# Token-major gates and branches, a ready-made convolution table, and a first block without splitting

## The chip, the cores and the metric

The kernel runs on one core of a Trainium2 chip. The metric is the device time of one execution in microseconds (us). The number reported is the median over runs.

## The reference

Two transformer blocks run one after the other on S = 256 tokens of width D = 2048, all in float32. What matters here, cut short:

```python
# first block: three branches, then a feed-forward
gates = sigmoid(gate_logits)                        # gate_logits = columns of rms_norm(x) @ w_in
mixed = (gates[0] * (o_a @ w_branch_a) + gates[1] * (o_b @ w_branch_b)
         + gates[2] * (o_c @ w_branch_c))
x = x + rms_norm(mixed @ w_out, g_post_mix)
h2 = rms_norm(x, g_pre_ffn)
f_gate, f_up = split(h2 @ w_ffn_in)
x = x + rms_norm((silu(f_gate) * f_up) @ w_ffn_out, g_post_ffn)
...
# second block, layer 0: a state-space mixer
h = modulate(rmsnorm(x), shift, scale)
u, z = split(h @ w_in)
x_re, x_im = scan(a_re, a_im, bu_re, bu_im)         # one recurrence per group and state, along tokens
y = einsum(x_re, c_re) - einsum(x_im, c_im) + d_skip * u
y = gelu(y); y = y * sigmoid(y @ w_glu + b_glu)
x = x + gate * ((y * silu(z)) @ w_out)
# second block, layer 1: attention over a shared key/value store
h_kv = modulate(rmsnorm(x), kv_shift, kv_scale); kv = h_kv @ w_kv
h = modulate(rmsnorm(x), shift, scale); proj = h @ w_qg; ...
```

## The kernel before

Nearly all of the work is products of a 256 x K operand with a weight of K x N. A weight is streamed in *units* of 256 rows x 512 columns (512 KB). For each unit, SyncE issues a load into one of four `raw` buffers. ScalarE then rounds it to the matmul's short format (`whi`, L156), and VectorE subtracts that from the original (`wlo`, L157). The activations are held as the same kind of pair (`Act`, parts `hi` and `lo`). A product is three matmuls: hi x hi, hi x lo and lo x hi. There are three `whi` and three `wlo` buffers.

A block is 512 output columns and, for K = 2048, eight units. Two orders exist. In `ws` (L190) the weights are stationary: a unit is 24 matmuls of 256 columns, and the output has the channels on the partitions. In `as_` (L223) the activations are stationary: a unit is 12 matmuls of 512 columns, and the output has the tokens on the partitions. After each unit, `pump` gives a turn to side work, which is written as generators: attention, retention, tables, modulation. The `credit` of a generator says how many steps it takes per unit. `self.late` holds steps that the next `as_` block runs after its second unit (third for K = 2048).

Three norms lie on the way: after the branches (`post_norm`, L830), after the feed-forward (`ffn`, L895, whose result goes to `ssm`) and after the state-space layer (`gated_out`, whose result goes to `nsa`). At each of them the last block or blocks are computed token half by token half (`as_last`, `by_tokens`, L254): in the pass t = 0 over tokens 0 to 127 the units are loaded and most of them kept in large buffers (`kept`), and in the pass t = 1 they are used again. So the norm of the first half can be worked out while the second half is multiplied. `by_tokens` keeps all units but the last three; those use `whi` and `wlo`. The first block after a norm (`as_first`, L301) is also done by halves, and `ready(k, t)` prepares two channel blocks of its operand at a time: transposes on TensorE (`tp`), scaling, and a split into a pair. In that block VectorE is busy with the norm, so GpSimd does the subtraction for the weights (`shared`, and the flag `True` in `as_first`). The factor of a norm is a chain of small VectorE operations on one column (`rstd`, L333 to L341), and in the last two norms also a diagonal matrix `diag` (L363) with which TensorE transposes and scales in one step.

The state-space layer's short convolution uses tables that depend on weights alone. `ssm_tables` makes them as side work during the feed-forward: tiles of `gm` are loaded, multiplied, and written by GpSimd's queue to a DRAM tensor `kern` of 128 groups (L1297, 32 issues). Later `ssm_direct` (L1577) loads 16 tiles of 8 groups with overlapping rows of 128 elements, and GpSimd zeroes what lies in the future by a product with a mask `past` (L1588). In that stretch TensorE computes z, and VectorE also runs the scan, four operations a step (L1545 to L1548).

The order on each engine is set by the tile framework's scheduler, from the order of the code, its own estimate of durations and the waits written as `issue_after`. DMAs go through the queues of SyncE and of GpSimd; within a queue they are issued in order.

## Time and profile before

| | |
|---|---|
| runs | 3265.74, 3266.39, 3269.41 us; median 3266.39 |
| profiled execution | 3265.34 us, of which the span is 3263.2 us |
| mean granted TensorE clock | 0.989 of full speed |
| busy over the span | TensorE 97%, its weight load 86%, VectorE 73%, ScalarE 45%, GpSimd 5% |
| DMA | 744.48 MB, 228 GB/s in the mean |

The span is what the trace covers; 2.1 us lie around it. A busy share is a mean over stages. TensorE's 97% leaves some 97 us in which it waits, and these lie in a few places. Its clock is granted at two levels, so the mean of 0.989 also stands for a few stretches at half speed.

### The profile page before, as it was taken

The numbers are of one execution on the slowest core, as the hardware profiler recorded it, in microseconds if no ns is written. First come the engines' busy times: TensorE is split into PE (matmuls) and PEld (weight loads), VectorE is DVE, ScalarE is ACT, GpSimd is POOL, SyncE is SP. The second block draws the span as 40 slices with busy tenths as digits, with TensorE's granted clock in tenths as the row PEclk, the third lists the DMA queues.
The fourth block names the chain that finished last, engine by engine and source line by source line (L and its number), as shares of the span: only waits on it lengthen the run. The fifth ranks groups of instructions, "written<-read, shape, count | busy, mean of one in ns | idle before, by whom it ended". The sixth has DMA issues, their size and how long they took to land. (4 is left out here: it accounts for less than half of the span.)

```text
span 3263.2 us, 52186 instructions
## 1 busy us (share of the span) xinstructions
PE 3166.2 (97%) x20582; PEld 2812.7 (86%) x20582; DVE 2375.1 (73%) x3580; ACT 1461.9 (45%) x2066; POOL 177.2 (5%) x184
## 2 busy tenths in 40 slices
PE   9999999999999998999999999898899899999998
PEld 8999899988999996887778778677798798899997
DVE  7777676777787766999989956757777865655666
ACT  5544434344344445444434444554444434544444
POOL 0000000000000002000000010303100200000000
PEclk9999999999999999999999999898999999999999
DMA  8868756888777785677777788486788585455574
GB/s 280 260 196 270 237 184 200 255 279 270 223 235 246 249 286 160 213 273 251 262 264 272 253 279 272 139 273 199 232 240 268 170 272 174 135 150 161 143 229 171
DMA packets 438246, 744.48 MB, mean 228 GB/s; under 512 B 29732, under 2 KB 105288, under 8 KB 437104
## 3 DMA queue, kind: packets, MB, share of 16 engines
q1 hardware_dynamic: 428000, 710.45, 68.4%
q0 software_dynamic: 9360, 29.62, 2.6%
q8 instruction: 161, 2.64, 0.3%
q10 hardware_dynamic: 640, 1.07, 0.1%
q14 instruction: 85, 0.70, 0.1%
HBM read 716.80 MB, written 24.24 MB: 227 GB/s over the span
## 5 line engine op out<-in xcount | busy, mean ns | idle before, releaser
L156 ACT CAST whi<-raw 128x1024 fp32r<-128x1024 f32 (+2 forms) x1059 | 1029.5, 981 | 1375.8 <-PE mm L150 1191.3
L157 DVE TENSOR_TENSOR wlo<-raw,whi 128x1024 fp32r<-128x1024 f32 (+2 forms) x1045 | 1181.6, 1139 | 611.3 <-ACT whi L156 600.0
L150 PE MATMUL mm<-act,whi 128*128 128x256 f32 (+1 forms) x8000 | 1485.0, 287 | 3.7 <-ACT whi L156 3.7
L150 PEld LDWEIGHTS mm<-act,whi 128*128 128x128 f32 (+1 forms) x8000 | 1255.5, 193 | 34.7 <-issue 24.3
L150 PE MATMUL mm<-whi,act 128*128 128x512 f32 x3792 | 1185.1, 391 | 5.4 <-ACT whi L156 4.5
L150 PE MATMUL mm<-act,wlo 128*128 128x256 f32 (+1 forms) x4000 | 1143.7, 288 | 7.0 <-DVE wlo L157 6.9
L150 PEld LDWEIGHTS mm<-whi,act 128*128 128x128 f32 x3792 | 711.4, 188 | 160.6 <-issue 7.0
L150 PEld LDWEIGHTS mm<-act,wlo 128*128 128x128 f32 (+1 forms) x4000 | 767.9, 193 | 23.9 <-issue 11.9
L150 PE MATMUL mm<-wlo,act 128*128 128x512 f32 x1896 | 743.9, 393 | 13.6 <-DVE wlo L157 11.6
L150 PEld LDWEIGHTS mm<-wlo,act 128*128 128x128 f32 x1896 | 356.6, 188 | 98.2 <-DVE wlo L157 21.3
L1087 DVE SCALAR_TENSOR_TENSOR acc<-side_raw,c_act,acc 128x512 f32<-128x512 f32 x480 | 359.3, 749 | 23.2 <-DMA side_raw<-mod_w 18.4
L150 PE MATMUL mm<-kept,act 128*128 128x512 f32 x360 | 95.0, 411 | 9.3 <-DVE act L157 9.3
L150 PEld LDWEIGHTS mm<-kept,act 128*128 128x128 f32 x360 | 69.1, 197 | 25.5 <-DVE act L157 10.9
L1273 DVE TENSOR_TENSOR side<-tables,ssm_c 128x512 f32<-128x512 f32 x64 | 65.7, 1088 | 2.3 <-DMA ssm_c<-ssm_c_re 2.3
L1107 POOL DMA_DIRECT2D mod<-side x24 | 12.0, 499 | 959.9 <-ACT side L1106 958.6
L156 ACT CAST kept<-raw 128x1024 fp32r<-128x1024 f32 x30 | 31.2, 1049 | 27.8 <-DMA raw<-w_out 7.4
L1588 POOL TENSOR_TENSOR side_raw<-side_raw,past 128x1024 f32<-128x1024 f32 x16 | 39.5, 2479 | 60.7 <-PE mm L150 33.5
L160 DVE SCALAR_TENSOR_TENSOR act<-tp,vec,act 128x256 fp32r<-128x256 f32 (+1 forms) x64 | 25.4, 413 | 22.3 <-ACT act L159 21.9
L150 PEld LDWEIGHTS tp<-diag,x 128*128 128x128 f32 x192 | 27.7, 205 | 15.1 <-issue 9.8
L150 PE MATMUL tp<-diag,x 128*128 128x128 f32 x192 | 29.0, 292 | 11.3 <-DVE diag L363 9.0
L159 ACT ACTIVATE act<-tp,vec 128x256 fp32r<-128x256 f32 (+1 forms) x64 | 25.5, 418 | 28.2 <-DVE act L160 13.4
L346 ACT ACTIVATE big<-x 128x512 f32<-128x512 f32 x40 | 25.1, 628 | 27.2 <-DVE x L1640 18.5
(378 smaller groups left out, 1929.8 us busy)
## 6 DMA issues: line engine op xcount, KB each, us to landing
raw<-w_in SPq DMA_DIRECT2D x272, 512.0 KB, 4.5
side_raw<-mod_w SPq DMA_DIRECT2D x192, 512.0 KB, 5.2
raw<-w_ffn_in SPq DMA_DIRECT2D x176, 512.0 KB, 5.0
raw<-nsa_w_qg SPq DMA_DIRECT2D x128, 512.0 KB, 3.7
raw<-w_ffn_out SPq DMA_DIRECT2D x88, 512.0 KB, 5.3
side_raw<-kv_mod_w SPq DMA_DIRECT2D x64, 512.0 KB, 4.7
raw<-ssm_w_in SPq DMA_DIRECT2D x64, 512.0 KB, 5.0
raw<-w_kv SPq DMA_DIRECT2D x48, 512.0 KB, 4.4
```

Source lines behind the costliest of these rows:

```text
L150: return self.nc.tensor.matmul(out, lhsT, rhs, start=start, stop=stop, skip_group_check=True).ins
L156: self.last_hi = nc.scalar.copy(hi, src).ins
L157: self.last = (engine or nc.vector).tensor_sub(lo, src, hi.bitcast(F32)).ins
L159: nc.scalar.activation(hi, src, AF.Copy, scale=scale)
L160: self.last_scaled = nc.vector.scalar_tensor_tensor(lo, src, scale, hi.bitcast(F32), op0=OP.mult, op1=OP.subtract).ins
L346: return self.nc.scalar.activation(self.work([128, 512], "big"), x, AF.Square, accum_out=out).ins
L1087: nc.vector.scalar_tensor_tensor(acc, raw[:, k], c, acc, op0=OP.mult, op1=OP.add)
L1107: nc.gpsimd.dma_start(flat[n:n + 4].rearrange("(o k) p -> o (k p)", o=1), row[r])
L1273: nc.vector.tensor_mul(w[i], y[r][:, :, :, None].to_broadcast([128, 4, 8, 16]), x[q][:, :, None, :].to_broadcast([128, 4, 8, 16]))
L1588: nc.gpsimd.tensor_mul(raw, raw, cols(past, 8))
```

## The change

Three parts.

1. `branch` uses `as_` instead of `ws`, for the gates and for the branch products: 160 units. `mixed` becomes two tiles of tokens x 2048 channels instead of channels x tokens. The operand of `w_out` is therefore made by transposes (`transpose_act`), put on `self.late` in the branch that comes last.
2. `as_first` no longer splits anything for its own block. The weights are loaded into large buffers as they are (`kept_raw`; two units use `raw`), the operand is kept unsplit (class `Unsplit`), and each product is one float32 matmul. The split of the operand, which the following blocks need, is done in the pass t = 1 of that block (`rest`). GpSimd splits no weights any more. The two `hold`s on the order of the splits and of the block's weights go away; that on `done` stays. Transposes of the first half are asked for inside `as_last` (`beside`).
3. `kern` holds for each of its 16 rows of a group 112 zeros and the values, so that the masked table can be copied out of it without a mask: 128 new DMAs on GpSimd's queue, one for each group, from `kern` to a DRAM tensor `direct` (64 KB each). `ssm_direct` loads plain tiles of `direct`, and its product with `past` is gone. The loads of `gm` in `ssm_tables` are fetched one ahead.

```diff
     def branch(self, i, o, w, mixed, act=None, done=None):
...
         for b in range(4):
-            ps = self.ws(self.hT, win, GATE + i * D + b * 512)
+            c = slice(b * 512, b * 512 + 512)
+            ps = self.as_(self.hT, win, GATE + i * D + b * 512)
...
-            ps = self.ws(o, wv, b * 512)
...
+            ps = self.as_(o, wv, b * 512)
+            for t in range(2):
+                m, g = mixed[t].t[:, c], gs[t]
...
-                if done is not None:
-                    self.split(done.hi(k, 2), done.lo(k, 2), m, 0.5)
+            if done is not None:
+                self.late.append(partial(self.transpose_act, [m.t[:, c] for m in mixed], done, 4, b * 4, 0.5))
```

```diff
+class Unsplit:
...
+    def rest(self, act):
+
+        def rest(k):
+            while act.n < k + 2:
+                act.grow()
+            self.k.split(act.hi(k, 2), act.lo(k, 2), self.slots[k // 8].t[:, k % 8:k % 8 + 2])
...
-    def as_first(self, act, wv, c0, ready):
+    def as_first(self, x, wv, c0, ready, rest):
...
+        slots, raws = [], []
+        for t in range(2):
             r = slice(t * 128, t * 128 + 128)
+            ready(0, t)
+            for u in range(8):
+                k0 = u * 2
+                if u < 7:
+                    ready(k0 + 2, t)
+                if t == 0:
+                    if u < 6:
+                        if u % 2 == 0:
+                            slots.append(self.slot([128, 2, 2, 512], F32, "kept_raw"))
+                        raw = slots[-1].t[:, u % 2]
+                    else:
+                        raw = self.wp.tile([128, 2, 512], F32, name="raw", bufs=4)
+                    self.nc.sync.dma_start(raw, self.rows_of(wv, k0)[:, :, c0:c0 + 512])
+                    raws.append(raw)
+                for k in range(2):
+                    self.mm(ps[t], x(k0 + k)[:, r], raws[u][:, k], k0 + k == 0, k0 + k == 15)
+                if t:
+                    rest(k0)
```

```diff
-        self.kern = dp.tile([128, 112 + 16 * 128], F32, name="kern")
+
+        self.kern = dp.tile([128, 16, 240], F32, name="kern")
+        self.direct = dp.tile([16, 128, 8, 128], F32, name="direct")
...
+            for g in range(t * 16, t * 16 + 16):
+                src = bass.AP(tensor=self.kern.tensor, offset=self.kern.offset + g * 3840, ap=[[240, 16], [16, 8], [1, 128]])
+                nc.gpsimd.dma_start(self.direct[g // 8, :, g % 8].rearrange("(c s) w -> c s w", s=8), src)
+            yield 0.1
...
-            nc.sync.dma_start(raw, bass.AP(tensor=self.kern.tensor, offset=self.kern.offset + g * 2160,
-                                           ap=[[16, 128], [2160, 8], [1, 128]]))
-            nc.gpsimd.tensor_mul(raw, raw, cols(past, 8))
+            nc.sync.dma_start(raw, self.direct[g // 8])
```

The scheduler moves work around these edits. Three places follow. Line numbers of before and after differ (L960 is L991, L157 is L180, L156 is L179, L346 is L378, L938 is L969, L1297 is L1334).

The first is VectorE at the end of the feed-forward, where the residual of the first token half is added (`x<-y,bit,x`). Before:

```order
L340 TENSOR_SCALAR bit<-bit 128x1
L341 SCALAR_TENSOR_TENSOR bit<-bit 128x1
L960 SCALAR_TENSOR_TENSOR x<-y,bit,x 128x512 x4
L371 TENSOR_REDUCE bit<-bit 128x1
L372 TENSOR_SCALAR bit<-bit 128x1
```

And now (`acc` is side work for the modulation):

```order
L372 TENSOR_SCALAR bit<-bit 128x1
L373 SCALAR_TENSOR_TENSOR bit<-bit 128x1
L991 SCALAR_TENSOR_TENSOR x<-y,bit,x 128x512 x2
L180 TENSOR_TENSOR wlo<-raw,whi 128x1024 x2
L1118 TENSOR_SCALAR acc<-side_raw,c_act 128x512
L1120 SCALAR_TENSOR_TENSOR acc<-side_raw,c_act,acc 128x512
L180 TENSOR_TENSOR wlo<-raw,whi 128x1024
L991 SCALAR_TENSOR_TENSOR x<-y,bit,x 128x512 x2
L403 TENSOR_REDUCE bit<-bit 128x1
L404 TENSOR_SCALAR bit<-bit 128x1
```

The four additions stood in one piece. Now three subtractions for the weights of the second state-space block stand between the first two and the last two. On ScalarE the casts for these units and the squares of `x` alternate in the same way:

```order
L378 ACTIVATE big,bit<-y 128x512 x2
L179 CAST whi<-raw 128x1024
L378 ACTIVATE big,bit<-x 128x512 x2
L179 CAST whi<-raw 128x1024 x2
L378 ACTIVATE big,bit<-x 128x512 x2
```

Before, the four squares of `x` stood in one row (`L346 ACTIVATE big,bit<-x 128x512 x4`), ahead of the casts.

The second place is GpSimd from the tables to the end of the feed-forward. Before (`y<-y,gb` scales the feed-forward's output, whose square has been taken, by the norm's gain):

```order
L1297 DMA kern<-side 16x4x128 x16
L1107 DMA mod_13956<-side 16x1x32 x2
L1297 DMA kern<-side 16x4x128 x16
L938 TENSOR_TENSOR y<-y,gb 128x512 x2
L157 TENSOR_TENSOR kept<-raw,kept 128x1024 x4
L938 TENSOR_TENSOR y<-y,gb 128x512 x2
L157 TENSOR_TENSOR kept<-raw,kept 128x1024
```

Now, from the last third of the tables on:

```order
L1334 DMA kern<-side 16x4x128
L1338 DMA direct<-kern 128x1x128 x32
L1334 DMA kern<-side 16x4x128
L1338 DMA direct<-kern 128x1x128 x12
L1334 DMA kern<-side 16x4x128 x2
L1338 DMA direct<-kern 128x1x128 x4
L1334 DMA kern<-side 16x4x128 x2
L969 TENSOR_TENSOR y<-y,gb 128x512 x2
L1338 DMA direct<-kern 128x1x128 x16
L969 TENSOR_TENSOR y<-y,gb 128x512 x2
```

The 128 new issues stand among the old ones and ahead of the products that the residual waits for; the splits of `kept` are gone.

The third is TensorE where the state-space layer's output (pass t = 1) meets the first block of `w_kv`. Before:

```order
L150 MATMUL tp<-diag,x 128x128 x4
L150 MATMUL mm_24443<-wlo,act 128x512
L150 MATMUL mm_24443<-whi,act 128x512 x2
L150 MATMUL mm_24443<-wlo,act 128x512
L150 MATMUL mm_24443<-whi,act 128x512
L150 MATMUL tp<-diag,x 128x128 x2
L150 MATMUL mm_24518<-kept,act 128x512 x2
L150 MATMUL tp<-diag,x 128x128 x2
L150 MATMUL mm_24518<-kept,act 128x512 x10
```

And now:

```order
L173 MATMUL tp<-diag,x 128x128 x4
L173 MATMUL mm_22417<-wlo,act 128x512
L173 MATMUL mm_22417<-whi,act 128x512 x2
L173 MATMUL mm_22417<-wlo,act 128x512
L173 MATMUL mm_22417<-whi,act 128x512
L173 MATMUL mm_22506<-kept_raw,unsplit 128x512 x2
L173 MATMUL tp<-diag,x 128x128 x2
L173 MATMUL mm_22506<-kept_raw,unsplit 128x512 x2
```

The first transposes stand at the same place. After them two matmuls on the unsplit operand stand between two pairs of transposes; before, it was two to ten on the split pair.

## Rows read from the trace of the kernel before

**Rows 1.** The page, part 1: busy time, share and instructions of each engine.

```profile
PE 3166.2 (97%) x20582; PEld 2812.7 (86%) x20582; DVE 2375.1 (73%) x3580; ACT 1461.9 (45%) x2066; POOL 177.2 (5%) x184
```

**Rows 2.** Stretches: start:end, length, busy PE, PEld, DVE, ACT, POOL, clock, DMA share, GB/s.

```profile
833.00:1001.00 168.00, 168.00 (x1312) 161.32 (x1312) 132.68 (x292) 67.58 (x81) 1.94 (x4) 1.00 0.71 222
1250.00:1310.00 60.00, 51.80 (x230) 38.92 (x229) 38.76 (x103) 32.88 (x74) 19.96 (x10) 1.00 0.41 122
2040.00:2090.00 50.00, 37.68 (x155) 30.03 (x154) 41.90 (x86) 25.78 (x55) 24.25 (x12) 0.83 0.44 139
2220.00:2330.00 110.00, 93.37 (x964) 83.28 (x964) 100.25 (x181) 47.74 (x77) 39.46 (x16) 0.92 0.72 215
2532.00:2580.00 48.00, 39.67 (x185) 32.73 (x184) 37.82 (x71) 21.38 (x43) 20.79 (x10) 0.89 0.54 184
1910.00:2045.00 135.00, 134.74 (x738) 109.15 (x738) 83.07 (x113) 71.54 (x92) 17.41 (x34) 1.00 0.83 273
```

**Rows 3.** The chain that ended last: start, us, what.

```profile
2740.76 0.87 PE tp L1901 x8
...
2870.83 0.86 PE pv L150 x2
...
2873.43 2.88 PE mm L150 x24
```

**Rows 4.** Timeline of PE at the plain float32 product of the last group.

```profile
2870.67 1.02 PE L150 MATMUL pv<-side,vsw 128*128 128x512 f32 x2
```

**Rows 5.** Timeline of ACT: first operation after a gate block of branch b, twice.

```profile
1017.19 0.60 ACT L815 ACTIVATE big<-mm 128x512 f32<-128x512 f32 x1 [0.51 <-PE mm L150]
...
1063.27 0.60 ACT L815 ACTIVATE big<-mm 128x512 f32<-128x512 f32 x1 [0.51 <-PE mm L150]
```

**Rows 6.** Timeline of ACT: first operation after two following blocks of `w_out`.

```profile
1201.73 0.60 ACT L346 ACTIVATE big<-mm 128x512 f32<-128x512 f32 x1 [0.53 <-PE mm L150]
...
1223.49 0.60 ACT L346 ACTIVATE big<-mm 128x512 f32<-128x512 f32 x1 [0.53 <-PE mm L150]
```

**Rows 7.** Groups of instructions on POOL: busy us, mean ns, idle before.

```profile
L1588 POOL TENSOR_TENSOR side_raw<-side_raw,past 128x1024 f32<-128x1024 f32 x16 | 39.5, 2479 | 60.7 <-PE mm L150 33.5 <-DMA side_raw<-kern 26.3 <-PE sc L150 0.8
L157 POOL TENSOR_TENSOR wlo<-raw,whi 128x1024 fp32r<-128x1024 f32 x14 | 34.4, 2474 | 32.4 <-ACT whi L156 28.2 <-issue 4.1
L157 POOL TENSOR_TENSOR kept<-raw,kept 128x1024 fp32r<-128x1024 f32 x10 | 23.5, 2365 | 7.3 <-ACT kept L156 7.3
```

**Rows 8.** Timeline of PE behind the feed-forward.

```profile
2066.90 2.05 PE L150 MATMUL tp<-diag,x 128*128 128x128 f32 x8 [7.55 <-DVE diag L363]
```

**Rows 9.** Timeline of DVE in the same wait.

```profile
2059.63 0.16 DVE L341 SCALAR_TENSOR_TENSOR bit<-bit 128x1 f32<-128x1 f32 x1
...
2062.43 1.96 DVE L341 SCALAR_TENSOR_TENSOR bit<-bit 128x1 f32<-128x1 f32 x1
```

**Rows 10.** The page, part 5: the operations that stand ahead of `diag` after the change.

```profile
L156 ACT CAST whi<-raw 128x1024 fp32r<-128x1024 f32 (+2 forms) x1059 | 1029.5, 981 | 1375.8 <-PE mm L150 1191.3
L157 DVE TENSOR_TENSOR wlo<-raw,whi 128x1024 fp32r<-128x1024 f32 (+2 forms) x1045 | 1181.6, 1139 | 611.3 <-ACT whi L156 600.0
...
L1087 DVE SCALAR_TENSOR_TENSOR acc<-side_raw,c_act,acc 128x512 f32<-128x512 f32 x480 | 359.3, 749 | 23.2 <-DMA side_raw<-mod_w 18.4
```

**Rows 11.** Timeline of DVE at the start of `nsa`.

```profile
2558.00 6.79 DVE L341 SCALAR_TENSOR_TENSOR bit<-bit 128x1 f32<-128x1 f32 x1
```

**Rows 12.** Waits between 2220 and 2330 us: sum, times, longest.

```profile
PEld sc L150 <- POOL side_raw L1588: 12.0, 4, 4.8
```

**Rows 13.** Instructions that write or read `kern`: ns min/median/max, first and last start.

```profile
L1297 POOL DMA_DIRECT2D kern<-side x32: 512/512/532, 1910.8 to 1978.3; - x32
...
L1245 POOL DMA_DIRECT2D kern<-half x1: 556/556/556, 1414.4 to 1414.4; - x1
```

**Rows 14.** Queues, of the DMA view: packets, MB, share of 16 engines over the span.

```profile
q0 software_dynamic: 9360, 29.62, 2.6%
```

**Rows 15.** Timeline of POOL at the end of the feed-forward.

```profile
2052.82 1.29 POOL L938 TENSOR_TENSOR y<-y,gb 128x512 f32<-128x512 f32 x1 [3.56 <-ACT big L346]
```

More of the change, by code (lines that the diff above doesn't have):

```diff
@@ L63, in free, with __init__, x @@
             t.free()
+class Unsplit:
+    def __init__(self, k):
+        self.k, self.slots = k, []
+    def x(self, i):
+        while len(self.slots) <= i // 8:
+            self.slots.append(self.k.slot([128, 8, S], F32, "unsplit"))
+        return self.slots[i // 8].t[:, i % 8]
+    def rest(self, act):
[3 more added lines that the diff above has]
+            self.k.split(act.hi(k, 2), act.lo(k, 2), self.slots[k // 8].t[:, k % 8:k % 8 + 2])
+            if k == 14:
+                for s in self.slots:
+                    s.free()
+        return rest
 class Slot:
@@ L252, in do_late, with by_tokens @@
             f()
-    def by_tokens(self, units, products, shared=False, beside=None):
+    def by_tokens(self, units, products, beside=()):
         kept = []
@@ L838, in post_norm @@
         ss, new = self.work([128, 2, 4], "bit"), self.work([128, 2, 4], "bit")
-        h2 = Act(self, 0)
-        r, beside = [], deque()
+        h2, unsplit = Act(self, 0), Unsplit(self)
+        r, there = [], set()
         def add(t, b, p):
@@ L852, in done @@
                     normed(i, 0)
-                for k in range(0, 16, 4):
-                    beside.append(partial(both, k))
         def normed(i, t):
@@ L859, in normed, with beside @@
             nc.vector.scalar_tensor_tensor(x, y[t].t[:, c], r[t], x, op0=OP.mult, op1=OP.add)
-        def both(k):
-            ready(k, 0)
-            ready(k + 2, 0)
+        def beside(u):
+            if u > 3:
+                ready(u * 2 - 8, 0)
         def ready(k, t):
-            while h2.n < k + 2:
-                h2.grow()
+            if (k, t) in there:
+                return
+            there.add((k, t))
             if t == 1 and k % 4 == 0:
-                with self.tc.issue_after(self.last_scaled) if k else nullcontext():
-                    normed(k // 4, 1)
+                normed(k // 4, 1)
             elif t == 1:
-                with self.tc.issue_after(self.last_hi):
-                    for i in range(2):
-                        self.square(xs[i].t[:, k // 4 * 512:k // 4 * 512 + 512], new[:, i, k // 4:k // 4 + 1])
+                for i in range(2):
+                    self.square(xs[i].t[:, k // 4 * 512:k // 4 * 512 + 512], new[:, i, k // 4:k // 4 + 1])
             p = self.ps([128, 2, 128], "tp", 2)
-            rows = slice(t * 128, t * 128 + 128)
             for j in range(2):
@@ L892, in post_norm, with ffn @@
         gb.free()
-        return xs, h2, partial(ready, t=1), new
-    def ffn(self, xs, h2, ready, ss):
+        return xs, h2, (unsplit.x, ready, unsplit.rest(h2)), new
+    def ffn(self, xs, h2, first, ss):
         nc, a = self.nc, self.a
@@ L1050, in first @@
         self.hT.free()
-        for m in mixed:
-            m.free()
         self.BACK = 0.2
-        xs, h2, ready, ss = self.post_norm(mx, a["w_out"], a["g_post_mix"], a["x"][0])
+        self.late += [m.free for m in mixed]
+        xs, h2, first, ss = self.post_norm(mx, a["w_out"], a["g_post_mix"], a["x"][0])
         mx.free()
@@ L1057, in first @@
         self.BACK = 0.3
-        operand = self.ffn(xs, h2, ready, ss)
+        operand = self.ffn(xs, h2, first, ss)
         self.finish(tables)
@@ L1443, in done, with beside @@
             ds.extend(self.diags(ss))
-            if t == 0:
-                self.hold, self.hold_act = self.last_diag, self.last_square
-                for k in range(0, 4, 2):
-                    operand[2](k, 0)
-        self.gated_out(g, a["ssm_w_out_2"].rearrange("o (k p) n -> p (o k) n", p=128), xs, 0, done)
+        def beside(u):
+            if u > 4 and u < 7:
+                operand[2][1](u * 2 - 10, 0)
+        self.gated_out(g, a["ssm_w_out_2"].rearrange("o (k p) n -> p (o k) n", p=128), xs, 0, done, beside)
         return operand
@@ L1648, in gated_out @@
                 add(t, b, ps[t])
-        self.as_last(act, wv, (3,), add)
+        self.as_last(act, wv, (3,), add, beside)
         gr.free()
@@ L1686, in nsa @@
         wq = a["nsa_w_qg_2"].rearrange("o (k p) n -> p (o k) n", p=128)
-        hk, n, ready = operand
+        hk, n, first = operand
         def shifted(act, i, k):
```

134 lines of the change are left out of this document (55 added, 79 removed).

## The prediction

> **What bounds the kernel now.** I read the busy times of the page first. TensorE is busy for 97% of the span [rows 1], so a change pays in two ways only: less time in matmuls, or less time in which TensorE waits or runs at half speed. The next view is the table of stretches [rows 2]. In 833 to 1001 us, a stretch of the branches, TensorE is busy for 168 of 168 us at full clock, and VectorE for 132.68. Four other stretches lose time. The loss of one is its idle time plus what the clock takes: one less the mean clock, times the busy time. That gives 8.2 us in 1250 to 1310 (the feed-forward begins), 12.3 + 6.4 = 18.7 us in 2040 to 2090 (the state-space layer begins), 16.6 + 7.5 = 24.1 us in 2220 to 2330 (the convolution's tables), and 8.3 + 4.4 = 12.7 us in 2532 to 2580 (`nsa` begins). The third view is the rows inside these stretches, which say who holds TensorE. In three of them it is VectorE: one-column operations that take 0.16 us elsewhere take 1.96 [rows 9] or 6.79 [rows 11] while GpSimd runs its 40 tensor operations of 2.4 to 2.5 us [rows 7]. In the tables it is the product with `past` [rows 12].
>
> **Branches by tokens: -22.1 us.** In branch b the first tanh of one gate block and that of the next lie 46.08 us apart, with 16 units between them, so 2.88 us for each [rows 5]. The chain has the same for 24 matmuls [rows 3]. For `w_out`, which already has activations stationary, a block of eight units is 21.76 us, 2.72 each [rows 6]. The branches have 160 units: 160 x 0.16 = 25.6 us less. New are 32 transposes of 0.109 us (eight took 0.87 [rows 3]), 3.5 us. What hides the rest: a cast of 0.98 and a subtraction of 1.14 us a unit [rows 10] are as many as before, and VectorE's share, 0.79 of 833 to 1001 [rows 2], rises to 0.84. If that cover fails in places I keep a loss of up to 7 us, so -15 to -24.
>
> **The unsplit first block.** A float32 matmul of 512 columns is two records [rows 4] and takes 0.86 us in the chain [rows 3]; a block has 32 of them, 27.5 us against 21.8, so each of three blocks costs 5.8 us more on TensorE. Against that stand the 24 weight splits that leave GpSimd [rows 7], and with them the long one-column operations.
>
> At the feed-forward the 8.2 us of idle time come in pieces, and each piece also drains and refills the pipeline, by about 0.16 us (two matmuls alone take 1.02 us, in a row 0.86 [rows 3, 4]); with ten pieces that is some 9.8 us. I leave 1.5 us of stall, since the operand of the second token half still waits for a factor on VectorE: -8.3 + 5.8 = **-2.5** (0 to -6).
>
> At the state-space layer the listing of VectorE's order decides. Three subtractions for weights now stand ahead of the last two additions to `x`, and the third of them needs the last `whi` buffer. The three units that are not kept hold these buffers to the end of the pass, T, and a unit of a half pass is 6 matmuls of 0.227 us, so the buffers come free at T - 2.7, T - 1.4 and T. ScalarE's order is one cast, two squares (0.6 us each [rows 6]), two casts (1.0 [rows 10]): the last ends at about T + 2.1. VectorE then does a subtraction (to T + 2.3), two steps of `acc` at 0.75 us [rows 10] (T + 3.8), the third subtraction (T + 5.0) and two additions (T + 6.4). The last square ends at T + 7.2, and the chain of small operations, some 2 us without GpSimd, at T + 9.3. So TensorE would idle about 9.4 us, where it idled 7.55 [rows 8]: VectorE's long operations go and a wait for buffers takes their place. With some 4 us for a clock that falls as it did before, and 5.8 for the block, 19.2 us stand against 18.7: **+0.5**. If the order did not bind, three operations of about 2 us would shrink to 0.2 [rows 9], and the loss would be near 9 us, -10; if the half clock lasts longer, +4.
>
> At `nsa` the first four transposes stand inside the pass t = 1, as before, and nothing holds VectorE: of 12.7 us I leave 1, and add 5.8: -5.9, rounded to **-5.5** (-1 to -7).
>
> **Tables without a mask: -17 us.** The 16 products of 2.48 us [rows 7] leave, and with them their hold on VectorE, which is busy 100.25 of 110 us there [rows 2]; at 2.1 us for each that is 34 us less. All of 24.1 us is the most that TensorE can win. Of this, 12.0 us is a wait for the product itself [rows 12]; I add two thirds of the 7.5 us of clock, since the stalls that precede the falls go. The rest stays, with the loads (as many bytes, in longer rows) and the scan as the next late things. Bounds: -5 to -24.
>
> **128 new DMAs: +3 us.** Their issue costs GpSimd 128 x 0.556 = 71 us (a DMA of 128 rows [rows 13]), on a queue that is nearly empty. With 32 issues of `kern` at 0.51, POOL has 79 us of work from 1910.8 on before the first `y<-y,gb`, which stood at 2052.82 [rows 13, 15]. Done without waits that is 1990; with 25 us for landings of `kern`, 2015, some 38 us early. The transfers are 8.39 MB. By the queue's 29.62 MB in 2.6% of 3263.2 us [rows 14] they are 24 us of all 16 engines, and between 1910 and 2045, at a share of 0.83, 23 us are free [rows 2]. Nearly all of it hides, if spread well; +3, from 0 to +25 if reading and writing both count. The `gm` loads fetched one ahead cost nothing: TensorE idles 0.26 us in that stretch.
>
> The SBUF page of the Trainium skill speaks against these DMAs. "SBUF — State Buffer", section "SBUF: two separate sides", says that GpSimd cannot write the descriptors of its DMAs while VectorE holds their shared port; the section after it, "A bandwidth-pool intuition that's wrong (but worth ruling out)", puts such a DMA at about 3.1 us. As an estimate from that page, the issues would take 128 x 3.1 = 397 us, and the kernel would end some 250 us later than in my sum. This trace does not agree for such issues: with VectorE busy 83 of 135 us [rows 2] the 32 issues took 512 to 532 ns [rows 13].
>
> **The sum.** -22.1 - 2.5 + 0.5 - 5.5 - 17 + 3 = -43.6. Against the profiled execution's 3265.3 us that is 3221.7; the median of the runs lies 1.05 us above it, so 3223.
>
> **Rivals.**
>
> 1. *The stalls go altogether* (0.2). The splits on VectorE don't bind (-10 for +0.5), the tables give all 24 us, the copies hide: 10.5 + 7 + 3 us less, about 3202. For it: GpSimd is the one common holder in all four stretches. Against it: the order above.
> 2. *The tables turn their wait into another* (0.17). With the product gone, the tiles wait for DMA (share 0.72 already, and the same bytes in less time) or VectorE's scan: 5 us in place of 17, about 3235.
> 3. *The copies push weight loads* (0.08). 24 us of transfer at either end, with the engines at 0.83: +25 in place of +3, about 3245. For it: the stretch's 273 GB/s is above the mean. Against it: its TensorE doesn't wait at all now, so loads run ahead. The same SBUF page, section "A bandwidth-pool intuition that's wrong (but worth ruling out)", gives 358 GB/s between HBM and a core. As an estimate from it, 36.9 MB of the stretch and 16.8 MB of copies, read and written, need 150 us, 15 more than now: 3235. No run here shows that limit yet.
> 4. *GpSimd is late* (0.03), the other side. If an issue of `direct` takes more than 0.556 + 38/112 = 0.9 us (112 stand ahead of the first `y<-y,gb`), the feed-forward's end waits for it. From 0.556 + (38 + 43.6 + 6.5)/112 = 1.35 us the kernel is slower than before by over 0.2%; at 1.5 us it would end at about 3290. Against it: the 512 to 556 ns of [rows 13]. The rule of the SBUF page above would be this case at its extreme, near 3470 by its figure.
>
> My own sum has 0.52. Its own range, from the bounds of single terms, is about 3212 to 3233. For 8 in 10 I take in rival 1 and most of rival 2: **3200 to 3240**. A measurement of this kernel tells about 0.2% (6.5 us) from no change. All cases but the fourth, and the worst of the second and third together, end faster: faster 0.95, same 0.02, slower 0.03.
>
> **What the next profile would show.** Branch blocks of 21.8 us between tanh groups, no long `bit` operations beside GpSimd, three first blocks of about 27.5 us. A wait of about 9 us for `diag` behind the feed-forward, still at half clock for a while. Some 93 us for the work that now takes 110 from 2220 on. `direct` issues of 0.5 to 0.6 us, done before `y<-y,gb` is due, and no weight load late in that stretch. I am wrong if VectorE, with subtractions closer together in the branches, makes TensorE wait, if that 9 us wait is far shorter, or if the tables still take over 105 us.

## The result, and the profile after

The changed kernel's runs gave 3216.06, 3216.18, 3218.44 and 3220.26 us, median 3217.31; the kernel before, on the same chip, had a median of 3267.9 us over four runs. The ratio is 0.9845, with a 95% interval of 0.9828 to 0.9862. The forecast was 3223 with a range of 3200 to 3240. The profiled execution took 3220.26 us, 44.9 us less than the profiled one of before; its span is 3218.4.

Page, part 1, after; to be read against [rows 1]:

```profile
PE 3140.6 (98%) x18598; PEld 2676.3 (83%) x18598; DVE 2312.8 (72%) x3556; ACT 1436.9 (45%) x2018; POOL 147.7 (5%) x272
```

TensorE is busy 25.6 us less, so 19 us of the 45 were waits. Some 13 of the 25.6 are clock, as an estimate: one less the mean granted clock, times the busy time, is 34.8 us before (0.989) and 22.0 after (0.993). The same stretches as in [rows 2], after (start:end, length, busy PE, PEld, DVE, ACT, POOL, clock, DMA share, GB/s):

```profile
816.00:980.00 164.00, 164.00 (x732) 132.55 (x731) 134.41 (x292) 68.42 (x81) 2.16 (x4) 1.00 0.75 234
1230.00:1290.00 60.00, 58.13 (x213) 37.38 (x213) 40.52 (x113) 27.58 (x59) 0.98 (x2) 0.97 0.43 143
2018.00:2068.00 50.00, 39.19 (x148) 26.96 (x148) 32.34 (x84) 19.47 (x43) 13.47 (x20) 0.86 0.50 165
2200.00:2290.00 90.00, 88.28 (x1009) 79.71 (x1008) 71.44 (x182) 49.80 (x81) 0.00 (x0) 1.00 0.84 278
2490.00:2535.00 45.00, 43.65 (x184) 30.20 (x184) 28.56 (x70) 16.17 (x30) 1.09 (x2) 1.00 0.63 222
1890.00:2022.00 132.00, 130.73 (x741) 104.36 (x741) 85.20 (x116) 73.39 (x95) 76.10 (x146) 1.00 1.00 347
```

The idle time of the feed-forward's start (8.2 us), of the tables (16.6 us) and of `nsa` (8.3 us) is down to 1 to 2 us, and the clock is full or nearly so. The stretch 2018 to 2068 still loses 10.8 us of idle time at a clock of 0.86. While the copies run, the DMA engines are full (share 1.00).

The same operation can be looked up in both traces. The starts of some that read a product of TensorE give the sum of all gains up to there:

| operation | before, us | after, us | difference | of it new |
|---|---|---|---|---|
| first square of `w_out`'s first block | 1201.73 | 1181.67 | -20.1 | -20.1 (branches) |
| product with `ffn_r`, first block of the feed-forward | 1328.25 | 1306.10 | -22.2 | -2.1 |
| last addition to `y`, pass t = 0 | 2051.23 | 2030.27 | -21.0 | +1.2 |
| copy of the second state-space block | 2127.97 | 2107.76 | -20.2 | +0.7 |
| product with the GLU's bias, first | 2395.26 | 2354.64 | -40.6 | -20.4 |
| first copy to `cmp_src` | 2614.73 | 2569.70 | -45.0 | -4.4 |

Behind the last of these little moves: the spans differ by 44.8 us. Each start is of one execution. From the product with `ffn_r` to the last addition to `y`, six kernels with the same code there, the changed one and five of those below, took 719.3 to 724.2 us, so a difference of 1 or 2 us in one row says little.

### The profile page after: what moved, and what is told of

Its sections match the earlier page's. It is cut to its first block, busy times and chain, and to the rows that moved or that the text cites. A ratio compares the mean times of both kernels' runs of the same rounds, so it can differ in the third digit from the quotient of the medians.

```text
span 3218.4 us, 48219 instructions
## 1 busy us (share of the span) xinstructions
PE 3140.6 (98%) x18598; PEld 2676.3 (83%) x18598; DVE 2312.8 (72%) x3556; ACT 1436.9 (45%) x2018; POOL 147.7 (5%) x272
## 5 line engine op out<-in xcount | busy, mean ns | idle before, releaser
L180 DVE TENSOR_TENSOR wlo<-raw,whi 128x1024 fp32r<-128x1024 f32 (+2 forms) x1045 | 1178.4, 1136 | 619.5 <-ACT whi L179 606.4
L179 ACT CAST whi<-raw 128x1024 fp32r<-128x1024 f32 (+2 forms) x1045 | 1015.9, 980 | 1341.7 <-PE mm L173 1150.3
L173 PE MATMUL mm<-whi,act 128*128 128x512 f32 x4960 | 1553.4, 392 | 7.7 <-ACT whi L179 7.7
L173 PEld LDWEIGHTS mm<-whi,act 128*128 128x128 f32 x4960 | 930.0, 188 | 213.7 <-issue 12.7
L173 PE MATMUL mm<-act,whi 128*128 128x256 f32 (+1 forms) x5440 | 1012.4, 287 | 4.1 <-ACT whi L179 4.1
L173 PE MATMUL mm<-wlo,act 128*128 128x512 f32 x2480 | 973.9, 393 | 15.0 <-DVE wlo L180 14.9
L173 PEld LDWEIGHTS mm<-act,whi 128*128 128x128 f32 (+1 forms) x5440 | 850.9, 192 | 27.4 <-issue 18.9
L173 PE MATMUL mm<-act,wlo 128*128 128x256 f32 (+1 forms) x2720 | 777.8, 288 | 2.5 <-DVE wlo L180 2.4
L173 PEld LDWEIGHTS mm<-wlo,act 128*128 128x128 f32 x2480 | 466.2, 188 | 124.2 <-DVE wlo L180 25.4
L173 PEld LDWEIGHTS mm<-act,wlo 128*128 128x128 f32 (+1 forms) x2720 | 519.2, 192 | 16.7 <-issue 11.0
L173 PE MATMUL mm<-kept_raw,unsplit 128*128 128x512 f32 x144 | 72.0, 621 | 3.6 <-DVE unsplit L910 1.9
L1338 POOL DMA_DIRECT2D direct<-kern x128 | 66.9, 541 | 24.9 <-DMA direct<-kern 13.2
L173 PEld LDWEIGHTS mm<-kept_raw,unsplit 128*128 128x128 f32 x144 | 26.1, 197 | 23.9 <-issue 13.5
L180 DVE TENSOR_TENSOR kept<-raw,kept 128x1024 fp32r<-128x1024 f32 x20 | 24.5, 1224 | 20.3 <-ACT kept L179 20.2
L378 ACT ACTIVATE big<-x 128x512 f32<-128x512 f32 x40 | 25.0, 625 | 24.8 <-DVE x L1671 17.6
```

The source lines that it names most:

```text
L173: return self.nc.tensor.matmul(out, lhsT, rhs, start=start, stop=stop, skip_group_check=True).ins
L179: self.last_hi = nc.scalar.copy(hi, src).ins
L180: self.last = (engine or nc.vector).tensor_sub(lo, src, hi.bitcast(F32)).ins
L378: return self.nc.scalar.activation(self.work([128, 512], "big"), x, AF.Square, accum_out=out).ins
L1338: nc.gpsimd.dma_start(self.direct[g // 8, :, g % 8].rearrange("(c s) w -> c s w", s=8), src)
```

## The wait behind the feed-forward

The longest wait that is left there reads, after, on TensorE's timeline (the bracket is the idle time before, and who ended it; to be read against [rows 8]):

```profile
2048.07 2.05 PE L173 MATMUL tp<-diag,x 128*128 128x128 f32 x8 [10.58 <-DVE diag L395]
```

VectorE's timeline in that wait:

```profile
2034.20 1.41 DVE L991 SCALAR_TENSOR_TENSOR x<-y,bit,x 128x512 f32<-128x512 f32 x2
2035.94 1.23 DVE L180 TENSOR_TENSOR wlo<-raw,whi 128x1024 fp32r<-128x1024 f32 x1 [0.32 <-ACT whi L179]
2038.11 1.23 DVE L180 TENSOR_TENSOR wlo<-raw,whi 128x1024 fp32r<-128x1024 f32 x1 [0.94 <-ACT whi L179]
...
2042.16 1.22 DVE L180 TENSOR_TENSOR wlo<-raw,whi 128x1024 fp32r<-128x1024 f32 x1 [1.64 <-ACT whi L179]
2043.30 1.41 DVE L991 SCALAR_TENSOR_TENSOR x<-y,bit,x 128x512 f32<-128x512 f32 x2
...
2047.63 0.29 DVE L395 TENSOR_SCALAR diag<-ident,bit 128x128 f32<-128x128 f32 x1
```

And ScalarE's third cast:

```profile
2041.08 1.04 ACT L179 CAST whi<-raw 128x1024 fp32r<-128x1024 f32 x1 [3.01 <-DMA raw<-ssm_w_in]
```

The one-column operations are short again, and `diag` takes 0.29 us. Before, two one-column operations took 1.96 us each, and `diag` 2.33, beside GpSimd's splits. The second of the two is in [rows 9]; the first, `diag` and the splits read, before:

```profile
2060.13 1.96 DVE L341 SCALAR_TENSOR_TENSOR bit<-bit 128x1 f32<-128x1 f32 x1
2064.42 2.33 DVE L363 TENSOR_SCALAR diag<-ident,bit 128x128 f32<-128x128 f32 x1
```

```profile
2059.73 9.26 POOL L157 TENSOR_TENSOR kept<-raw,kept 128x1024 fp32r<-128x1024 f32 x4 [5.63 <-ACT kept L156]
```

But now three subtractions for the second state-space block stand between the two pairs of additions, and the last pair starts 9.1 us after the first. The forecast had the third cast wait for the last `whi` buffer. It waited for its load, and the load for another buffer: SyncE issued it when the first of the three subtractions was done and a `raw` buffer came free. Of the four, two held units of the first block (L342) and two the first units of the second (L202). SyncE's timeline:

```profile
2019.90 2.70 SPq L342 DMA_DIRECT2D raw<-ssm_w_in  x2
2023.97 2.10 SPq L202 DMA_DIRECT2D raw<-ssm_w_in  x2
2037.19 2.54 SPq L202 DMA_DIRECT2D raw<-ssm_w_in  x2
```

## The experiments

Each was timed in five rounds beside the kernel before. Ratios are to that kernel, with 95% intervals; the changed kernel has 0.9845 [0.9828, 0.9862].

**Each part alone.** Three kernels, each with the hunks of one part and nothing else.

> Only the branches are changed (activations stationary, 32 transposes). If the gain is TensorE's own time, the landmark behind the branches (first square of w_out's first block, at 1201.7 us before) comes 20 to 22 us earlier and all later ones keep that distance: about 3246, ratio 0.9935. If VectorE or ScalarE cannot keep up with shorter units, the landmark moves by 15 us or less. If the shift is lost again later in a wait for data, the end moves by less than 15 although the landmark moved by 20.

Measured: 3248.2 us, 0.9944 [0.9932, 0.9957]. The landmark is at 1181.51, 20.2 us earlier. Timeline of ScalarE at the first two blocks of `w_out`, in this run:

```profile
1181.51 0.60 ACT L346 ACTIVATE big<-mm 128x512 f32<-128x512 f32 x1 [0.53 <-PE mm L150]
...
1203.27 0.60 ACT L346 ACTIVATE big<-mm 128x512 f32<-128x512 f32 x1 [0.53 <-PE mm L150]
```

The 21.76 us from one block to the next is that of [rows 6], and TensorE is busy for all of 816 to 980 in the changed kernel: VectorE keeps up at 134.41 of 164 us. By the sum it should have been 22.1; 2 us of it were not found.

> Only the tables are changed (128 copies, no product with the mask, gm fetched one ahead); GpSimd still splits weights in the first blocks. My reading of the two traces: the stretch of the tables gives about 20 us and the copies cost about 1, so about 3247, ratio 0.994. Rival: part of the 20 us comes from what the other two parts changed (what GpSimd does, other arrival times), then 10 us or less here.

Measured: 3249.4 us, 0.9943 [0.9931, 0.9956]. The total was as expected, but not the places. At the state-space layer's start this run is 10 to 13 us *later* than before, and at the last block of z 17.4 us earlier, so the tables' stretch gave some 28 us. GpSimd's timeline where the loss begins, and ScalarE's casts for the same splits:

```profile
2053.29 8.39 POOL L1305 DMA_DIRECT2D direct<-kern  x16
2061.58 4.75 POOL L157 TENSOR_TENSOR kept<-raw,kept 128x1024 fp32r<-128x1024 f32 x2
```

```profile
2057.87 3.87 ACT L156 CAST kept<-raw 128x1024 fp32r<-128x1024 f32 x4
```

Sixteen copies, 8.4 us of the queue, stand ahead of the weight splits that the next block waits for. The first split starts some 2.7 us after its cast is done, and the last of the eight ends at 2093.4 us, 7.8 us later than before. That these copies make the whole loss is argued from this order; no run moves them alone. In the changed kernel GpSimd has no splits to delay. So the third part loses here without the second part's new first block, and I had not seen that.

> Only the first blocks behind the norms are changed. By the landmarks of the two traces it gives 2 us at the feed-forward, loses 0.7 at the state-space layer and gives 4.4 at nsa: about 3260, ratio 0.998. If the three parts only add, this with the other two makes the 45 us between the profiled executions; if this part alone is slower than before, some of its gain needs the other parts.

Measured: 3260.16 us, 0.9978 [0.9969, 0.9987], as expected. One place was not: from the last addition to `y` to the copy of the second state-space block this run is 2.7 us shorter than before, where 0.7 us of loss was expected. In this kernel the four additions to `x` stand in one piece, and the wait for `diag` is 7.23 us. The three parts alone make 0.0056 + 0.0057 + 0.0022 = 0.0135; all of them make 0.0155. The intervals allow both a plain sum and a little more.

**The wait for `diag`.** Splits of the next block behind the norm, on VectorE and ScalarE:

```diff
             if t == 0:
                 self.hold = self.last_diag
+                self.x_first = self.last_diag, last_square
...
             if q:
-                ps = self.as_(h, wi, q * 512)
+                diag, square = self.x_first
+                with self.tc.issue_after(diag), self.tc.issue_after(square):
+                    ps = self.as_(h, wi, q * 512)
```

> The changed kernel, with the splits of the second state-space block queued behind the squares and the diag of the first token half, on ScalarE and VectorE. If the 10.6 us wait for diag comes from those three splits, it falls to some 3 to 4 us, the half clock behind it gets shorter, and the kernel ends 6 to 10 us earlier: about 3209, ratio to before 0.9825. Rival: the norm's chain would take that long anyway (no move, ratio 0.9845). Second rival: the splits are late then, and TensorE waits for them in the second block instead (again near 0.9845, the wait moved).

Measured: 3210.14 us, 0.9827 [0.9814, 0.9841]. TensorE's timeline in this run:

```profile
2033.63 2.04 PE L173 MATMUL tp<-diag,x 128*128 128x128 f32 x8 [2.82 <-DVE diag L395]
```

10.58 us became 2.82, and the kernel's median 7 us less. The intervals of the two ratios overlap, so the total alone would not settle it; the row does. The order was the cause. Some of it moved: from these transposes to the copy of the second state-space block this run takes 2.8 us more.

**No copies.** The lines that issue the copies are left out, and the load reads `gm`:

```diff
-            nc.sync.dma_start(raw, self.direct[g // 8])
+            nc.sync.dma_start(raw, self.gm.rearrange("(t p) r (n m) w -> t (p r n) m w", t=16, m=8)[g // 8])
```

> The changed kernel without the 128 copies; the convolution loads its tiles from gm instead (as many bytes, wrong numbers), so this leaves out making the masked table. If the copies hide, as their stretch says (all 16 DMA engines full for 110 us, TensorE idle 1.3 us), the kernel gains 1 to 3 us: about 3215, ratio to before 0.984. Rival: they delay the first loads of the state-space layer, and with that the diag chain by some 5 us: about 3210.

Measured: 3207.99 us, 0.9813 [0.98, 0.9827], so the rival's number. In this run the stretch of the copies and the wait for `diag` read:

```profile
1890.00:2022.00 132.00, 131.74 (x755) 105.79 (x754) 85.22 (x114) 71.13 (x92) 17.47 (x34) 1.00 0.90 295
```

```profile
2039.20 2.05 PE L173 MATMUL tp<-diag,x 128*128 128x128 f32 x8 [7.40 <-DVE diag L395]
```

The DMA share falls from 1.00 to 0.90 and TensorE's idle time from 1.27 to 0.26 us; the wait for `diag` is 3.2 us shorter. But the rival's cause, a late load, is not what made it so. In both runs the load for the third cast is issued 0.3 us before TensorE's last product, and VectorE's third subtraction starts 4.6 to 4.7 us after that product. What differs is the order: without the copies the scheduler leaves the four additions in one piece, ahead of the subtractions:

```profile
2027.61 2.74 DVE L991 SCALAR_TENSOR_TENSOR x<-y,bit,x 128x512 f32<-128x512 f32 x4
```

So the run leaves out more than the copies, and its 9.3 us between the medians are not the price of their transfers. The rest lies in later waits that this run has shorter (for u, 2.5 in place of 5.5 us, and for `gm`): from the copy of the second state-space block to the first product with the GLU's bias it takes 239.1 us, the changed kernel 246.9. The next run, with every copy made twice, takes 241.2 there, so it isn't the copies by themselves that set these waits; what does stays open.

**Copies twice.** Each group is copied a second time, to a tensor that nobody reads:

```diff
-                nc.gpsimd.dma_start(self.direct[g // 8, :, g % 8].rearrange("(c s) w -> c s w", s=8), src)
+                for d in (self.direct, self.again):
+                    nc.gpsimd.dma_start(d[g // 8, :, g % 8].rearrange("(c s) w -> c s w", s=8), src)
```

> The changed kernel with each copy made twice, the second into a tensor that nobody reads: 128 more issues of 0.54 us (69 us of GpSimd's queue) and 8.39 MB more. GpSimd was done 24 us before its first product for the residual, and the DMA engines were already full. If GpSimd's lateness sets the price, TensorE waits for y scaled by the gain at the end of the feed-forward, some 35 us: about 3252. If the transfers set it, TensorE waits for weight loads in the feed-forward, some 20 to 25 us: about 3240. If there is room for both, under 3225.

Measured: 3269.15 us, 1.0002 [0.9993, 1.001]: all of the gain is lost. Two stretches of this run, then GpSimd's queue, then its issues (busy us, mean ns, idle before):

```profile
1890.00:2030.00 140.00, 138.19 (x768) 111.38 (x768) 83.74 (x113) 69.73 (x91) 95.85 (x184) 1.00 1.03 357
2030.00:2095.00 65.00, 2.03 (x10) 1.45 (x9) 13.46 (x34) 6.59 (x13) 55.91 (x105) 0.55 0.57 150
```

```profile
2087.46 2.61 POOL L969 TENSOR_TENSOR y<-y,gb 128x512 f32<-128x512 f32 x2
```

```profile
L1340 POOL DMA_DIRECT2D direct<-kern x128 | 75.6, 591 | 16.3 <-DMA direct<-kern 9.5 <-DMA kern<-side 4.0 <-issue 2.5
L1340 POOL DMA_DIRECT2D again<-kern x128 | 75.6, 590 | 25.7 <-DMA again<-kern 19.6 <-issue 5.6
```

While the copies run, TensorE again loses next to nothing (1.8 us of 140). What costs is that `y<-y,gb` comes at 2087 where it came at 2025: TensorE stands still for 63 us, where 35 were expected. Each issue took 0.59 us in place of 0.54, and the queue stood 29.1 us (9.5 + 19.6) until earlier copies had landed, so the transfers have a share in its lateness. This is the forecast's fourth rival, forced. In the changed kernel the queue was done 24.1 us ahead.

**GpSimd beside VectorE, with nobody waiting.** First with the tile of the table as operand:

```diff
             nc.sync.dma_start(raw, self.direct[g // 8])
+            for i in range(0, 8, 2):
+                nc.gpsimd.tensor_mul(spare, raw[:, i:i + 2], raw[:, i:i + 2])
             return raw
```

> The changed kernel with GpSimd squaring every table tile into a scratch tile that nobody reads (64 operations, a quarter tile each, together as much as the 16 products that went). If the loss in the tables' stretch came from GpSimd holding VectorE, VectorE's operations grow again and the stretch loses 6 to 15 us: 3223 to 3232. If it came from TensorE's wait for the product, nothing waits here, and the time stays at 3217 within 3 us.

Measured: 3235.5 us, 0.9901 [0.9886, 0.9916], 18 us more than the changed kernel. But TensorE's waits for tiles in this run (sum, times, longest) leave a doubt, since the tiles' buffers come free later:

```profile
PE pv L173 <- DMA side_raw<-direct: 6.9, 4, 3.2
...
PE sc L173 <- DMA side_raw<-direct: 3.4, 4, 1.4
```

So the same with a piece of the finished result as operand, 64 operations of the same size:

```diff
             nc.scalar.copy(self.y_groups(y, t), p)
+            part = y[t // 4].t[:, 0:4, t % 4 * 64:t % 4 * 64 + 64]
+            for i in range(8):
+                nc.gpsimd.tensor_mul(spare, part, part)
```

> As the run with the idle product, but GpSimd's 64 operations read a finished piece of the convolution's result and not the table tile, so no buffer of a tile waits for them; their result is read by nobody. If GpSimd's hold on VectorE makes the loss, it is there again: 3227 to 3235, with VectorE's scan operations longer than 0.3 us. If the loss of 18 us came from tiles that GpSimd held back (TensorE waited 12.1 us for tiles there), the time goes back to 3217 to 3222.

Measured: 3233.97 us, 0.9894 [0.9879, 0.991]. VectorE's scan (busy us, mean ns, idle before): two of its four operations from 2220 to 2330 in the kernel before, two from 2200 to 2290 in the changed kernel, and all four from 2195 to 2305 in this run:

```profile
L1548 DVE TENSOR_TENSOR state<-state,half 128x128 f32<-128x128 f32 x30 | 17.0, 565 | 0.8
L1545 DVE TENSOR_TENSOR half<-state,tables 128x128 f32<-128x128 f32 x30 | 16.3, 543 | 0.8
```

```profile
L1581 DVE TENSOR_TENSOR half<-state,tables 128x128 f32<-128x128 f32 x30 | 8.7, 290 | 0.8
L1584 DVE TENSOR_TENSOR state<-state,half 128x128 f32<-128x128 f32 x30 | 8.7, 290 | 0.8
```

```profile
L1583 DVE TENSOR_TENSOR state<-state,half 128x128 f32<-128x128 f32 x30 | 15.5, 517 | 0.1
L1581 DVE TENSOR_TENSOR half<-state,tables 128x128 f32<-128x128 f32 x30 | 15.4, 512 | 0.8
L1584 DVE TENSOR_TENSOR state<-state,half 128x128 f32<-128x128 f32 x30 | 15.0, 501 | 0.8
L1582 DVE TENSOR_TENSOR half<-state,tables 128x128 f32<-128x128 f32 x30 | 8.9, 295 | 0.0
```

Three of the four operations take 0.51 us in place of 0.29, and 17 us are lost though no one waits for GpSimd's result. The doubt is smaller but not gone: TensorE waits 5.3 us for tiles here. How much of the tables' stretch this is can be read from the time between ScalarE's first operation on the first block of z and that on the last:

| kernel | GpSimd beside it | first to last block of z, us |
|---|---|---|
| before; branches alone; unsplit alone | 16 products, awaited | 124.8; 124.6; 126.0 |
| changed; tables alone; no copies | nothing | 97.0; 96.7; 97.5 |
| squares of tiles; squares of the result | 64 squares, not awaited | 114.6; 116.0 |

As stretches (columns as in [rows 2]), before and changed, with the same 1027 matmuls:

```profile
2225.77:2350.58 124.81, 102.89 (x1027) 91.84 (x1025) 104.34 (x183) 49.80 (x76) 39.46 (x16) 0.91 0.73 214
2209.41:2306.42 97.01, 91.95 (x1027) 83.56 (x1025) 73.98 (x183) 50.48 (x76) 0.00 (x0) 1.00 0.86 274
```

The product's 27.8 us come back by 17.6 and 19.0, some two thirds, with nobody waiting for GpSimd. The squares are 50 us of GpSimd's time and the products were 39.5, so two thirds may be a little much. In this kernel the product with the mask cost more by what it did to VectorE than by being waited for. The Trainium skill, "SBUF — State Buffer", section "SBUF: two separate sides", has the mechanism: a GpSimd operation that reads SBUF and a VectorE operation with two SBUF inputs exclude each other for a whole operation. The rows of the wait behind the feed-forward agree: the two long one-column operations there have two inputs, and each ends within 0.1 us of the end of a split on GpSimd.

**Splits by VectorE.** The kernel before, with GpSimd's splits moved:

```diff
-        self.by_tokens(units, products, True)
+        self.by_tokens(units, products, False)
...
-                ps = self.as_(h2, wi, f * 512, before=None if f else self.ahead(ready), shared=f == 0)
+                ps = self.as_(h2, wi, f * 512, before=None if f else self.ahead(ready))
```

> The kernel before with one thing changed: in the three first blocks the weights are split by VectorE (24 subtractions of 1.14 us, 27 us more of its work) and not by GpSimd. If GpSimd's hold on VectorE made the waits of 8 to 19 us at the three norms, those waits shrink although VectorE has more to do: some 10 us less, about 3256. If GpSimd took work off a busy VectorE, as it was meant to, this is slower: 3270 to 3280. If both are even, 3264 to 3269, and then the unsplit block gains by needing no splits at all.

Measured: 3254.56 us, 0.9957 [0.9944, 0.9969]: 13.5 us less with 27 us more work on VectorE. TensorE's timeline behind the feed-forward, where 7.55 us stood [rows 8], and VectorE's:

```profile
2060.47 1.85 PE L150 MATMUL tp<-diag,x 128*128 128x128 f32 x8 [1.91 <-DVE diag L363]
2068.63 2.08 PE L150 MATMUL tp<-diag,x 128*128 128x128 f32 x8 [6.32 <-DVE half L1350]
```

```profile
2061.43 6.76 DVE L157 TENSOR_TENSOR kept<-raw,kept 128x1024 fp32r<-128x1024 f32 x4
```

The first wait is 5.64 us shorter. That is what the three long operations of the kernel before took over their time without GpSimd: 1.80 + 1.80 + 2.04 us. The splits still hold up the second transposes for 6.32 us, now as plain work. The unsplit block takes that away but pays, by the forecast's working, 5.8 us for each block on TensorE, and alone it gives less (0.9978) than this one. Of the 13.5 us, what comes from the shorter hold and what from splits of 1.2 us in place of 2.4 was not separated.

**The regrouping of u.** In the changed kernel ScalarE stands at the copies to `u_group`, which wait for their data, and three casts come behind them (ScalarE's timeline, changed kernel):

```profile
2125.07 3.86 ACT L1510 COPY u_group<-u_chunk 64x1024 f32<-64x1024 f32 x2 [9.68 <-DMA u_chunk<-u]
2128.78 2.99 ACT L179 CAST whi<-raw 128x1024 fp32r<-128x1024 f32 x3
```

Two tries on top of the splits behind `diag`. The first, with three `yield`s more ahead of the copies to `u_group` (`range(7)` for `range(4)`):

> The kernel with the splits behind diag (about 3210), and the regrouping of u taken up three units later. In the changed kernel TensorE waits 7.5 and 5.5 us because ScalarE stands at the regrouping, whose data comes through DRAM, with casts queued behind it. If that is the cause, both waits go: 8 to 13 us less, about 3199, ratio to before 0.979. Rival: the states and tables behind it are late in turn, and the gain is 3 us or less.

Measured: 3220.72 us, 0.9855 [0.9842, 0.9869], 10 us more than without. It did not test what it was to test: ScalarE's half of the regrouping stood where it was, with waits of 7.0 and 5.2 us, and only VectorE's half came later, and with it the scan. The second try:

```diff
-        for _ in range(4):
+        for _ in range(6):
             yield self.side[0][1]
...
-                (nc.vector.tensor_copy if j else nc.scalar.copy)(o, src)
+                with self.tc.issue_after(self.last_hi):
+                    (nc.vector.tensor_copy if j else nc.scalar.copy)(o, src)
```

> The kernel with the splits behind diag (about 3210), and the regrouping of u taken up two units later on both ScalarE and VectorE; in the last such try only VectorE's half had moved, and ScalarE still stood at it. If ScalarE's place in the queue makes the waits of 7.0 and 6.6 us, both shrink by some 5 us and the kernel ends at 3200 to 3206. If what follows (states, tables) is late in turn, as in the last try, 3210 or more.

Measured: 3203.08 us, 0.9801 [0.9788, 0.9815]. Of the wait for casts 1.8 us are left, and the wait for u is gone. So the cause holds. By the last block of z the run is 19 to 23 us ahead of the one without; by the product with the GLU's bias only 4.8 us of it are left. TensorE waits for tiles of `gm` there (6.2 us), but it does so without the edit too (7.8 us). How much of the lead was side work put off, and how much is lost again in waits, was not separated.

**All together, with VectorE's splits.** Parts one and three of the change, the edit that moves the splits to VectorE, and this regrouping:

> Branches by tokens, tables without a mask and the later regrouping of u, but the first blocks split as in the kernel before, with VectorE in GpSimd's place. Alone, the unsplit block gave 7 us and VectorE's splits 13 us, so this should end some 6 us before the same kernel with unsplit blocks (3203.1): 3194 to 3200. If the unsplit block's shorter work on VectorE is what the other parts need (its splits late behind 128 copies and the tables' side work), 3203 to 3210.

Measured: 3201.57 us, 0.9797 [0.9781, 0.9812]. That lies between the two ranges that were expected. Against 0.9801 [0.9788, 0.9815] with unsplit blocks and the splits behind `diag` it is no difference. Both beat the changed kernel, whose interval begins at 0.9828.

## Why the prediction was right, step by step

The sum of the forecast was -43.6 us against the profiled execution, and -44.9 was measured. Its terms:

| term | forecast | by landmarks |
|---|---|---|
| branches | -22.1 | -20.1 |
| first block of the feed-forward | -2.5 | -2.1 |
| first block of the state-space layer | +0.5 | +0.7 |
| first block of `nsa` | -5.5 | -4.4 |
| tables | -17 | -20.4, with a loss at u inside |
| copies, up to the end of the feed-forward | +3 | +1.2 |

*Branches.* Right, and shown by the kernel with them alone (-20.2 at the same place).

*Unsplit first blocks.* Right in each place. The order on VectorE, read before the run, gave a wait of 9.4 us for `diag`; it was 10.58, and moving the splits made it 2.82. One link was wrong: the third split waited 1.64 us for a load that needed a `raw` buffer, not for the last `whi` buffer. The order is not the second part's alone: with that part alone, or without the copies, the four additions stand in one piece, and the wait is 7.23 and 7.40 us. That GpSimd's hold on VectorE made the old wait behind the feed-forward is shown by the kernel that moves its splits to VectorE: the wait shrinks by just what the three long operations had taken beyond their usual time. For the start of the feed-forward it isn't: TensorE's idle time there came in pieces, some of them waits for GpSimd's splits themselves.

*Tables.* Mis-sized, and the cause was weighed wrongly. From the first to the last block of z the gain is 27.8 us, not 17, and more than the 24.1 that the forecast took for the most. Its stretch ended at 2330 us, ahead of the last block; up to that block the kernel before loses, by the forecast's way of counting, 21.9 us of idle time and 9.3 of clock, and the changed kernel 5.1 in all. The forecast took 12.0 of 17 us from TensorE's wait for the product. The runs with idle work on GpSimd lose 17.6 and 19.0 of the 27.8 us again with no such wait, so most of it was the hold on VectorE. By landmarks the 20.4 us also include two losses, 3.9 us ahead of the first block of z and 3.5 behind the last. Ahead of it TensorE waits 7.48 us for casts at 2122, behind ScalarE's regrouping of u, where it waited 4.28 before. The kernel with unsplit blocks alone has 6.45 there, so it comes with that part; I had not forecast it. The loss behind the last block stays open.

```profile
2129.93 1.22 PE L173 MATMUL mm<-whi,act 128*128 128x512 f32 x2 [7.48 <-ACT whi L179]
```

*Copies.* What the transfers cost is not shown beyond the 1 us of their stretch. Without the copies the kernel is 9.3 us faster between medians, within the bounds of 0 to 25 that the forecast had kept, but 3.2 us of that is the order on VectorE, and the rest lies in waits that are as short with twice the copies. The +1.2 of the table is within the spread of that row. The issues were as forecast, 0.54 us each; their waits for the DMA queue are new (idle time before, by releaser):

```profile
L1338 POOL DMA_DIRECT2D direct<-kern x128 | 66.9, 541 | 24.9 <-DMA direct<-kern 13.2 <-DMA kern<-side 7.2 <-issue 3.7
```

That the sum came out within 2 us is luck in part: the tables' stretch gave 10.8 us more than forecast, and 7.4 us of losses beside it, with 3.1 us less from the branches and `nsa`, took nearly as much back.

*The rivals.* The first (no stall at all, 3202) did not come: the order bound. Its time was reached in the end, at 3202 to 3203, with that order and the regrouping changed. The second was wrong: the tables' stretch is at 88.28 of 90 us. The third was half right: the engines are full, at 347 GB/s in the mean of 1890 to 2022, but TensorE idles only 1.27 us there. The fourth did not come by itself, and the doubled copies showed its mechanism.

The forecast's estimate of 397 us for the issues did not come true: 128 issues took 541 ns in the mean beside a VectorE that was busy for 85 of 132 us. The Trainium skill, "SBUF — State Buffer", section "A bandwidth-pool intuition that's wrong (but worth ruling out)", gives its 3.1 us for a DMA of GpSimd beside a VectorE `tensor_copy`. VectorE made no such copy in these 132 us (48.8 us of its time were the subtractions), so the figure isn't tested here. The same section of the Trainium skill gives 358 GB/s between HBM and a core. That was no limit here: this 20 us stretch of the changed kernel moved more, copies within DRAM included.

```profile
1950.00:1970.00 20.00, 20.00 (x116) 16.17 (x115) 13.24 (x15) 7.98 (x9) 14.42 (x29) 1.00 1.05 396
```

## What to carry to other kernels

When work is given to GpSimd to relieve VectorE, look for VectorE operations that are ten times too long beside it: here 24 splits of 2.4 us on GpSimd cost 13.5 us more than the same splits on a busy VectorE. Read each engine's order around the place where a norm or a factor is waited for; three operations for a later block in the midst of a chain can be seen before a run, priced by durations of the trace, and moved by one edit. Before more DMAs are put on a queue, list what stands behind them on it and by when it is needed: twice the copies cost 52 us, nearly all of it in one wait for an operation that stood behind them, and TensorE lost less than 2 us while they ran. And when a run leaves something out, compare the engines' orders before its time is called a price: without the copies VectorE's order changed too.

## What was not expected

VectorE's operations stretch with GpSimd's: beside operations of 2.4 us some took about 2, beside operations of 0.79 us (the idle squares) three of four took 0.5. With all 16 DMA engines at a share of 1.00 for 132 us, TensorE lost 1.3 us of them. And parts that are each timed as faster can get in each other's way or out of it: with the copies alone GpSimd's splits end 7.8 us later, and the unsplit block removes these splits; but only the two together bring the order that holds `diag` back for 10.58 us.
